# A Mamba-2 layer in split fp32: all weight splits at high priority, plain work inside the first Strassen pair, and another order of the scan's inserts

## The chip, the cores and the metric

The kernel runs on one core of one Trainium2 chip. The metric is the device time of one execution in microseconds (us). A core has a matmul engine (PE, or TensorE, with its weight load PEld), a vector engine (DVE), an activation engine (ACT), GpSimd (POOL) and SyncE (SP), which here mostly issues DMAs. Each engine runs its own instructions in a fixed order and waits on semaphores for the others.

## The reference

One Mamba-2 layer for 512 tokens and 2048 channels, with a final norm:

```python
hn   = rmsnorm(x, ln_g)
proj = hn @ w_in                        # 2048 -> z 4096, x 4096, B 1024, C 1024, dt 64
xbc  = silu(causal_conv4(x, B, C))
dt   = softplus(dt + dt_bias);  a = -exp(a_log)
# scan by chunks, 64 heads of 64 channels, 8 groups share B and C (128 states)
decay  = exp(where(mask, cs_l - cs_s, -inf));  cb = C @ B^T
y_diag = (cb * decay) @ (x * dt)
y_off  = (C @ state) * exp(cs)
state  = state * exp(last) + (B * w_in)^T @ (x * dt)
y = (y_diag + y_off + d_skip * x) * silu(z)
out = rmsnorm(x_in + rmsnorm(y, norm_g) @ w_out, final_g)
```

All inputs are float32.

## The kernel before, in words

**Splitting.** A float32 product is made of three matmuls on float32r parts: a weight piece arrives raw by DMA, ACT casts it to `hi` (L87) and DVE subtracts to get `lo` (L88); then hi*xh, hi*xl and lo*xh are summed in PSUM. The function is `split_piece`. Raw pieces lie in buffers `ra` (3), `rb` (1) and `rc` (2); `hi` and `lo` cycle through three buffers each, so a cast has to wait until PE is done with the piece three before it. A few splits have buffers of their own (`h1h`/`h1l` for R11, `oh`/`ol` in the out-projection).

**Stages.** First eight products ("plain": B0, C0, x0, z0, x1, z1, B1, C1) of 16 k-steps, in pieces of eight k-steps, through `mm_k` (L198). Then 36 *quads*: each computes two output tiles of the in-projection by a Strassen-Winograd scheme of seven half-size products, R11, T1, T2, R22, R21, T3 and T4, of 24 matmuls each (L635 to L637 for hi*xh, hi*xl, lo*xh). T1 is R12 fetched by DMA onto R11's raw buffer, T2 = T1 + R22 and T4 = T2 + R21 are made in place by DVE (L604), T3 is fetched onto R12. A quad's T4 product runs inside the next quad, behind T1: that place is called `prev`. Last come the out-projection's blocks: plain ones (`mm_o`, L929 to L931, 512 columns each, summed to `acc` by DVE at L1032), and two *chains* of four pairs each, `opair`, which use the same seven products (L867 to L869) on forms of y that `y_forms` makes on DVE (L841 to L848).

**The first pair of a chain.** The first quad, and the first pair of each out-projection chain, has no T4 of a predecessor for its `prev` place. There the order was another: T1, R11, nothing, R22, T2 (`lone`), and the events of the split moved with it.

**Order.** The code is traced in a loop of steps: a step is six matmuls (some 0.7 us), a quad is 28 steps. A table `ev` tells at which step a piece is loaded, split, added, or a part of the scan inserted; `add` fills it and `run` empties it. The order on PE, SP and POOL is the order in which the code was written and traced. The order on ACT and DVE is made by a scheduler, which takes what is ready in its own reckoning by priority; `with urgent():` gives instructions a high priority. Before, weight splits were urgent in the out-projection's pairs alone (L589).

**The scan.** For each of 32 units (two heads): `u_load` (DMA of decay rows), `u_decay` (ACT L456 to L459, then DVE L461 makes `m`), `u_xt` (transposes at L473, `xd` at L476, `xw` at L479), `u_state` (L488), `u_yd` (L502, L506, reads `m` and `xd`) and `u_yo` (L518 to L523). `g_bt` and `g_cb` prepare the groups (L416, L433 to L436). These are inserted between PE's steps. Around the start stand the token norm (L289 to L295), `dt` (L318 to L351) and `x_forms` (L549 to L578), which make the forms of x that the quads multiply with.

## Time and profile before

| what | value |
|---|---|
| median of 3 runs | 1290.69 us (1289.58 to 1293.99) |
| the profiled execution | 1295.7 us, its span 1294.0 us |
| granted PE clock, mean | 0.991 |
| PE busy | 1252.1 us (97%), 9932 matmuls |
| DVE busy | 1084.3 us (84%) |
| ACT busy | 826.6 us (64%) |
| POOL busy | 77.5 us (6%) |
| DMA | 225.90 MB, mean 175 GB/s |

The span is that of one execution, from its first to its last instruction. A row of the waits names the engine that stood still, its line and tile, and what ended its wait. A row of the timeline gives the start, the duration, the engine, the line, the operation, the tiles and, in brackets, the idle time before it. A row of the windows gives a stretch of the span, with the busy time of PE, PEld, DVE, ACT and POOL, and the clock that PE was granted. `L198 <- DVE lo L88` means a matmul of line 198 that waited for the difference of line 88.

### The profile page before, as it was taken

Reading aid. Unit: us, or ns where it says so; the run is one execution under the profiler, and the core shown is the slowest. Engines: PE = TensorE matmul, PEld = TensorE weight load, DVE = VectorE, ACT = ScalarE, POOL = GpSimd, SP = SyncE. Lnnn points to the kernel's source line nnn. Section 1 sums busy time; section 2 is a strip of 40 time slices with the busy share of each in tenths; the row PEclk is TensorE's granted clock in tenths of the full one; section 3 lists DMA queues with packets and bytes.
Section 4 is the critical chain, followed back from the end, with each engine's and each line's share of the span. In section 5 each row is a group of like instructions: output and inputs, shape, how many; then the busy total and the mean of one; then the engine's idle time right before and its main releaser. Section 6 shows DMA issues by size and latency. Waiting matters only on the chain.

```text
span 1294.0 us, 24519 instructions
## 1 busy us (share of the span) xinstructions
PE 1252.1 (97%) x9932; PEld 1192.9 (92%) x9932; DVE 1084.3 (84%) x1449; ACT 826.6 (64%) x1357; POOL 77.5 (6%) x99
## 2 busy tenths in 40 slices
PE   8989899999999999999999999999999899999997
PEld 8989899999999999999999999999988899899885
DVE  5796988988989898998889899889857877887865
ACT  7667667677666757767685867778666445434433
POOL 0000001010000101010100001000000000000000
PEclk9989999999999999999999999999999999999999
DMA  9546657585676667667667677766637576647612
GB/s 356 179 141 172 162 161 174 143 215 142 192 197 174 159 169 183 164 176 199 162 161 195 151 188 171 212 155 154 185 105 258 146 199 199 197 119 229 183 57 98
DMA packets 70194, 225.90 MB, mean 175 GB/s; under 512 B 8384, under 2 KB 12800, under 8 KB 69952
## 3 DMA queue, kind: packets, MB, share of 16 engines
q1 hardware_dynamic: 56688, 176.34, 40.2%
q0 software_dynamic: 12672, 46.14, 22.1%
q8 instruction: 78, 1.28, 0.4%
q10 hardware_dynamic: 720, 1.84, 0.4%
q14 instruction: 36, 0.29, 0.1%
HBM read 211.52 MB, written 12.78 MB: 173 GB/s over the span
## 4 chain that ended last, share of the span: by engine, by line
PE 74%; DVE 11%; DMA 7%; issue 4%; ACT 3%; SPq 0%; POOL 0%; DVEq 0%; ACTq 0%; POOLq 0%
PE S L637 7%; PE S L635 7%; PE S L636 7%; PE mm L635 5%; PE mm L636 4%; PE R L635 4%; PE mm L637 4%; PE R L636 4%; PE R L637 4%; DVE lo L88 3%; PE mm L929 3%; PE mm L931 3%; PE mm L930 3%; PE yd L502 2%; PE mm L867 2%
## 5 line engine op out<-in xcount | busy, mean ns | idle before, releaser
L87 ACT CAST hi<-ra 128x1024 fp32r<-128x1024 f32 x150 | 154.7, 1046 | 159.5 <-DVE ra L604 72.9
L88 DVE TENSOR_TENSOR lo<-ra,hi 128x1024 fp32r<-128x1024 f32 x150 | 181.3, 1221 | 24.2 <-ACT hi L87 24.1
L635 PE MATMUL mm<-xh,hi 128*128 128x256 f32 x576 | 163.6, 284 | 0.0
L637 PE MATMUL mm<-xh,lo 128*128 128x256 f32 x576 | 160.6, 279 | 0.6 <-DVE lo L88 0.6
L636 PE MATMUL mm<-xl,hi 128*128 128x256 f32 x576 | 160.4, 278 | 0.0
L637 PE MATMUL R<-s,lo 128*128 128x256 f32 x576 | 160.3, 278 | 0.1
L635 PE MATMUL R<-s,hi 128*128 128x256 f32 x576 | 160.2, 278 | 0.0
L636 PE MATMUL R<-s,hi 128*128 128x256 f32 x576 | 160.2, 278 | 0.0
L88 DVE TENSOR_TENSOR lo<-rc,hi 128x1024 fp32r<-128x1024 f32 x94 | 114.9, 1223 | 28.5 <-ACT hi L87 28.1
L87 ACT CAST hi<-rc 128x1024 fp32r<-128x1024 f32 x94 | 98.4, 1047 | 50.8 <-issue 29.1
L604 DVE TENSOR_TENSOR ra<-ra,rc 128x1024 f32<-128x1024 f32 x88 | 107.7, 1224 | 13.3 <-DMA rc<-in_wi 11.8
L635 PEld LDWEIGHTS mm<-xh,hi 128*128 128x128 f32 x576 | 108.1, 188 | 5.2 <-issue 5.0
L637 PEld LDWEIGHTS mm<-xh,lo 128*128 128x128 f32 x576 | 109.2, 190 | 0.8 <-DVE lo L88 0.8
L637 PEld LDWEIGHTS R<-s,lo 128*128 128x128 f32 x576 | 109.1, 189 | 0.3 <-DVE lo L88 0.3
L635 PEld LDWEIGHTS R<-s,hi 128*128 128x128 f32 x576 | 108.2, 188 | 0.0
L636 PEld LDWEIGHTS mm<-xl,hi 128*128 128x128 f32 x576 | 108.2, 188 | 0.0
L636 PEld LDWEIGHTS R<-s,hi 128*128 128x128 f32 x576 | 108.1, 188 | 0.0
L637 PE MATMUL S<-xh,lo 128*128 128x256 f32 x288 | 83.5, 290 | 5.6 <-DVE lo L88 5.6
L635 PE MATMUL S<-xh,h1h 128*128 128x256 f32 x288 | 83.4, 290 | 1.0 <-DVE xr L398 1.0
L635 PE MATMUL S<-xh,hi 128*128 128x256 f32 x288 | 81.3, 282 | 2.2 <-ACT xh L577 1.3
L636 PE MATMUL S<-xl,hi 128*128 128x256 f32 x288 | 81.2, 282 | 0.7 <-DVE xl L578 0.7
L636 PE MATMUL S<-xl,h1h 128*128 128x256 f32 x288 | 80.8, 280 | 0.0
(452 smaller groups left out, 3940.8 us busy)
## 6 DMA issues: line engine op xcount, KB each, us to landing
rc<-in_wi SPq DMA_DIRECT2D x76, 512.0 KB, 5.9
ra<-in_wi SPq DMA_DIRECT2D x42, 512.0 KB, 6.2
rb<-in_wi SPq DMA_DIRECT2D x40, 512.0 KB, 6.9
ra<-in_wi POOLq DMA_DIRECT2D x36, 512.0 KB, 6.3
rb<-in_wi POOLq DMA_DIRECT2D x36, 512.0 KB, 5.9
csb<-cscr SPq DMA_DIRECT2D x32, 512.0 KB, 8.0
ra<-in_wo SPq DMA_DIRECT2D x26, 512.0 KB, 5.4
yscr<-xs SPq DMA_DIRECT2D x32, 256.0 KB, 2.6
```

The lines of the kernel that those rows point to most:

```text
L87: S.copy(out=hi, in_=raw)
L88: V.tensor_tensor(out=lo, in0=raw, in1=hi, op=ALU.subtract)
L502: T.matmul(pyd[r, i, :], x[:, 2 * i, hh, :], m[:, i, hh::4, :], start=i == 0, stop=False, skip_group_check=True)
L604: V.tensor_tensor(out=raw, in0=raw, in1=qs[n][other], op=ALU.add)
L635: T.matmul(ps, hi[:, k, :], ah, start=first and k == 0, stop=False, skip_group_check=True)
L636: T.matmul(ps, hi[:, k, :], al, start=False, stop=False, skip_group_check=True)
L637: T.matmul(ps, lo[:, k, :], ah, start=False, stop=k == KH - 1, skip_group_check=True)
L867: T.matmul(ps[:, t, :], yh[:, k, tt], hi[:, k, :], start=st, stop=False, skip_group_check=True)
L929: T.matmul(ps, yh, hi, start=first and k == 0, stop=False)
L930: T.matmul(ps, yh, lo, start=False, stop=False)
L931: T.matmul(ps, yl, hi, start=False, stop=last and k == 1)
```

## The change

Three things are changed.

1. In `split_piece` the cast and the difference are now inside `urgent()`, for every weight piece of the kernel. (The lines are 89 and 90 there, and what follows is shifted by two to four lines.)
2. The first pair of a chain uses the same order as all others: R11, T1, `prev`, T2, R22, R21, T3. For `prev` it takes plain work: in the first quad the last four k-steps of the last plain product (so quads begin four steps earlier, `QB`), and in the out-projection the last two token tiles of the last piece of the block before the chain (`bridge`, made by `tail`, whose accumulate is L993). The offsets of `y_fetch` and `y_forms` for the first chain change, and the pieces that go to the pool's own buffers are those with n divisible by 4.
3. The events are added to the table in another order: within one step, yd now comes before `g_bt` and `g_cb`, and the state after them. On PE a steady insert `L488 L502 L506` becomes `L502 L506 L488` (in the lines of before).

```diff
--- before.py
+++ after.py
@@ -84,8 +85,9 @@
     def split_piece(raw, shape, pool, names=("hi", "lo"), bufs=None):
         hi = pool.tile(shape, F32R, name=names[0], bufs=bufs)
         lo = pool.tile(shape, F32R, name=names[1], bufs=bufs)
-        S.copy(out=hi, in_=raw)
-        V.tensor_tensor(out=lo, in0=raw, in1=hi, op=ALU.subtract)
+        with urgent():
+            S.copy(out=hi, in_=raw)
+            V.tensor_tensor(out=lo, in0=raw, in1=hi, op=ALU.subtract)
         return hi, lo
 
     def rsqrt_small(dst, ssq, pool, n, width, tag, bufs=1):
@@ -114,13 +116,14 @@
         seq.append((("x", u), ("z", u)))
     plain = [s for pair in (seq[0], seq[1], seq[2], seq[3]) for s in pair]
     quads = seq[NPL // 2:]
+    QB = NPL * KT - 4
     tile_of = {"z": 0, "x": 32, "B": 64, "C": 72}
     QS = 28
     at = {s: i * KT for i, s in enumerate(plain)}
     for i, pair in enumerate(quads):
         for s in pair:
-            at[s] = NPL * KT + i * QS
-    END = NPL * KT + len(quads) * QS
+            at[s] = QB + i * QS
+    END = QB + len(quads) * QS
     WSH = [P, 8, P]
     OSH = [P, 2, L]
 
@@ -140,6 +143,7 @@
     base = [END]
     for i, blk in enumerate(blocks):
         late = 4 if i == 0 or type(blocks[i - 1]) is tuple else 0
+        late -= 4 if type(blocks[min(i + 1, len(blocks) - 1)]) is tuple else 0
         base.append(base[-1] + (4 * QS if type(blk) is tuple else 8 * n_pieces(blk) + late))
 
     def wo_src(p, s):
@@ -160,7 +164,7 @@
     def get_out(n, name="ra"):
         if n < len(wo_order) and n not in opieces:
             opieces[n] = split_piece(load_piece(wo_src(*wo_order[n]), OSH, name), OSH,
-                                     *((op, ("oh", "ol")) if n % 4 == 3 else (wp,)))
+                                     *((op, ("oh", "ol")) if n and n % 4 == 0 else (wp,)))
 
 
     xh = xp.tile([P, KT, L], F32R, name="xh")
@@ -586,8 +590,7 @@
 
     def q_split(n, f, own=False):
         raw = qs[n][f]
-        with urgent() if n >= len(quads) else ExitStack():
-            qs[n, f] = split_piece(raw, WSH if n < len(quads) else QSH, wp, *((("h1h", "h1l"), 1) if own else ()))
+        qs[n, f] = split_piece(raw, WSH if n < len(quads) else QSH, wp, *((("h1h", "h1l"), 1) if own else ()))
 
     def q_load(n, f, half, tile_, name):
         qs.setdefault(n, {})[f] = load_piece(*q_src(n, half, tile_), name)
@@ -607,12 +610,11 @@
     qs = {}
     oquads = [blk for blk in blocks if type(blk) is tuple]
 
-    def q_events(n, b, last, e=0, t1=0, lone=False):
+    def q_events(n, b, last, e=0):
         for o, f, a in ((-38 - e, q_load, ("R11", 0, 0, "ra")), (-23 - e, q_split, ("R11", True)),
-                        (-23 - e, q_fetch, ("T1", "R11", 0, 1)), (-3 - e // 2 - t1, q_split, ("T1",)),
+                        (-23 - e, q_fetch, ("T1", "R11", 0, 1)), (-3 - e // 2, q_split, ("T1",)),
                         (-12 - e // 2, q_load, ("R22", 1, 1, "rc")), (1 - e // 2, q_add, ("T2", "T1", "R22")),
-                        *(((5, q_split, ("R22",)), (9, q_split, ("T2",))) if lone else
-                          ((5, q_split, ("T2",)), (9, q_split, ("R22",)))),
+                        (5, q_split, ("T2",)), (9, q_split, ("R22",)),
                         (-8, q_load, ("R21", 1, 0, "rc")), (12, q_add, ("T4", "T2", "R21")),
                         (13, q_split, ("R21",)),
                         (-7, q_load, ("R12", 0, 1, "rb")), (-7, q_fetch, ("T3", "R12", 1, 1)),
@@ -646,35 +648,17 @@
         W = lambda f: lambda: qs[n, f]
         A = ps_mm.tile([P, L], F32, name="mm")
 
-        def first(step):
-            product(s_, W("R11"), 11, True, step)
-            with urgent():
-                S.copy(out=A[:, lo_], in_=s_)
-
-        def second(step):
-            product(r_, W("T1"), 1, True, step)
-            with urgent():
-                S.copy(out=sn[:, 1, :], in_=r_)
-
-        if prev:
-            first(b)
-            second(b + 4)
-            prev(b + 8)
-        else:
-            second(b)
-            first(b + 4)
-            for i in range(8, 12):
-                run(b + i)
-        def third(step):
-            product(r_, W("R22"), 4, False, step)
-
-        def fourth(step):
-            product(s_, W("T2"), 2, False, step)
-            with urgent():
-                S.copy(out=sn[:, 0, :], in_=s_)
-
-        for f, step in zip((fourth, third) if prev else (third, fourth), (b + 12, b + 16)):
-            f(step)
+        product(s_, W("R11"), 11, True, b)
+        with urgent():
+            S.copy(out=A[:, lo_], in_=s_)
+        product(r_, W("T1"), 1, True, b + 4)
+        with urgent():
+            S.copy(out=sn[:, 1, :], in_=r_)
+        prev(b + 8)
+        product(s_, W("T2"), 2, False, b + 12)
+        with urgent():
+            S.copy(out=sn[:, 0, :], in_=s_)
+        product(r_, W("R22"), 4, False, b + 16)
         with urgent():
             V.tensor_tensor(out=zq[:, lo_], in0=r_, in1=sn[:, 0, :], op=ALU.add)
         product(A[:, lo_], W("R21"), 12, False, b + 20)
@@ -704,17 +688,23 @@
     def add(step, f, *a):
         ev.setdefault(step, []).append((f, a))
 
+    ramp = [[66, 71, 63, 75, 87, 92], [56, 65, 50, 68, 86, 92]]
+    steps = [ramp[u] if u < len(ramp) else [28, 42, 56, 65, 65, 71] for u in range(NU)]
+
+    def add_units(*kinds):
+        for u in range(NU):
+            for i, f in kinds:
+                add(at["x", u] + steps[u][i], f, u)
+
+    add_units((0, u_load), (1, u_decay), (2, u_xt))
+    add_units((4, u_yd))
     for g in range(1, G):
         add(at["B", g] + (30 if ("B", g) in plain else 93), g_bt, g)
         for i in range(2):
             add(at["x", 4 * g] + 28, g_cb, g, i)
-    ramp = [[66, 71, 63, 75, 87, 92], [56, 65, 50, 68, 86, 92]]
-    for u in range(NU):
-        w = ramp[u] if u < len(ramp) else [28, 42, 56, 65, 65, 71]
-        for o, f in zip(w, (u_load, u_decay, u_xt, u_state, u_yd, u_yo)):
-            add(at["x", u] + o, f, u)
+    add_units((3, u_state), (5, u_yo))
     for n in range(len(quads)):
-        q_events(n, NPL * KT + n * QS, n == len(quads) - 1, 0 if n else 14, lone=not n)
+        q_events(n, QB + n * QS, n == len(quads) - 1, 0 if n else 14)
     for i in range(4):
         add(49 + 7 * i, x_forms, i // 2, i % 2)
         add(114 + 4 * i, x_form3, i)
@@ -788,7 +778,7 @@
 
     for n in range(2, NPL):
         ps = None
-        for k in range(KT):
+        for k in range(KT if n < NPL - 1 else KT - 4):
             if k % 8 == 0:
                 get_piece(2 * n + k // 8 + 2)
             run(n * KT + k)
@@ -800,9 +790,15 @@
                 del pieces[2 * n + k // 8]
         if n == 2:
             st["x0"] = ps
-        else:
+        elif n < NPL - 1:
             finish(n, ps)
-    prev = None
+
+    def prev(step):
+        for i in range(4):
+            run(step + i)
+            mm_k(ps, pieces[2 * NPL - 1], 4 + i, KT - 4 + i)
+        finish(NPL - 1, ps)
+
     for n in range(len(quads)):
         prev = pair(n, prev)
 
@@ -878,36 +874,18 @@
         q0, q1 = acc[:, 0:2, c[1]], acc[:, 2:4, c[1]]
         A0 = ps_mm.tile([P, 2, LH], F32, name="mm")
 
...
+        oproduct(s_, i, W("R11"), 11, True, b)
+        with urgent():
+            S.copy(out=A0, in_=s_)
+        oproduct(r_, i, W("T1"), 1, True, b + 4)
+        with urgent():
+            V.tensor_tensor(out=q1, in0=q1, in1=r_, op=ALU.subtract)
+        prev(b + 8)
+        oproduct(s_, i, W("T2"), 2, False, b + 12)
+        with urgent():
+            V.tensor_tensor(out=q0, in0=q0, in1=s_, op=ALU.subtract)
+        oproduct(r_, i, W("R22"), 4, False, b + 16)
+        V.tensor_tensor(out=q0, in0=q0, in1=r_, op=ALU.subtract)
         oproduct(A0, i, W("R21"), 12, False, b + 20)
         V.tensor_tensor(out=p0, in0=p0, in1=A0, op=ALU.add)
         oproduct(s_, i, W("T3"), 3, False, b + 24)
@@ -963,10 +941,10 @@
     for i, blk in enumerate(blocks):
         if type(blk) is tuple:
             for s in range(4):
-                q_events(len(quads) + 4 * m + s, base[i] + s * QS, s == 3, 0, 3 if s == 0 else 0, s == 0)
+                q_events(len(quads) + 4 * m + s, base[i] + s * QS, s == 3)
             for j in range(2):
-                add(base[i] - ((50, 32), (54, 32))[m][j], y_fetch, m, j)
-                add(base[i] - ((39, 24), (47, 24))[m][j], y_forms, m, j)
+                add(base[i] - ((48, 30), (54, 32))[m][j], y_fetch, m, j)
+                add(base[i] - ((36, 23), (47, 24))[m][j], y_forms, m, j)
             m += 1
     sb = [i for i, blk in enumerate(blocks) if type(blk) is tuple]
     for i in range(16):
@@ -1006,6 +984,16 @@
                 step += QS
             m += 1
             continue
+        def tail(ps, w, y, t, s, first, step):
+            for k in range(2):
+                run(step + k)
+            mm_o(ps, w, y, t, first, True)
+            a = acc[:, t, s * L:(s + 1) * L]
+            with urgent():
+                V.tensor_tensor(out=a, in0=ps, in1=a, op=ALU.add)
+
+        bridge = []
+        n_end = n0 + n_pieces(blk)
         end = n0 + n_pieces(blk) + (n_pieces(blocks[kb + 1]) if kb + 2 < len(blocks) else 0)
         for s, pairs in blk:
             ps = [None] * NC
@@ -1018,6 +1006,9 @@
                     if p == pairs[0]:
                         ps[t] = first.pop(0) if first else (ps_o or (ps_s, ps_mm)[t % 2]).tile(
                             [P, L], F32, name="mm" if ps_o or t % 2 else "S")
+                    if type(blocks[kb + 1]) is tuple and s == 3 and n0 + 1 == n_end and t > 1:
+                        bridge.append(partial(tail, ps[t], opieces[n0], ys[p], t, s, p == pairs[0]))
+                        continue
                     if kb or n0 or t > 1:
                         for k in range(2):
                             run(step)
@@ -1043,6 +1034,10 @@
                     load_y(2)
                     fg = fp.tile([P, DM], F32, name="fg")
                     nc.sync.dma_start(fg, d["fg"].partition_broadcast(P))
+        if bridge:
+            def prev(step, parts=bridge):
+                for i, f in enumerate(parts):
+                    f(step + 2 * i)
 
 
     assert not ev, ev
```

The order on DVE shows what the scheduler makes of it. First, a quad behind a B/C pair, around the T3 difference (`lo<-rb`); L391 is the convolution, `m<-m,cbm` L461. Before:

```order
L88 TENSOR_TENSOR lo<-rc,hi 128x1024
L391 SCALAR_TENSOR_TENSOR xs<-xr,par,xs 128x512 x2
L461 TENSOR_TENSOR m<-m,cbm 128x1536
L391 SCALAR_TENSOR_TENSOR xs<-xr,par,xs 128x512
L679 TENSOR_TENSOR z<-R,sn 128x256
L88 TENSOR_TENSOR lo<-rb,hi 128x1024
L88 TENSOR_TENSOR lo<-ra,hi 128x1024
L604 TENSOR_TENSOR ra<-ra,rc 128x1024
```

Now (L395, L465 and L663 are what L391, L461 and L679 were):

```order
L90 TENSOR_TENSOR lo<-rc,hi 128x1024
L395 SCALAR_TENSOR_TENSOR xs<-xr,par,xs 128x512 x3
L90 TENSOR_TENSOR lo<-rb,hi 128x1024
L663 TENSOR_TENSOR z<-R,sn 128x256
L90 TENSOR_TENSOR lo<-ra,hi 128x1024
L607 TENSOR_TENSOR ra<-ra,rc 128x1024
L90 TENSOR_TENSOR lo<-ra,hi 128x1024
L465 TENSOR_TENSOR m<-m,cbm 128x1536
```

The T3 difference has moved ahead of `m<-m,cbm` and of the `z` that reads R. Second, the token norm at the start; `z<-ident,rtok` is made four times and read by PE at L294 (`tr`). Before:

```order
L102 TENSOR_TENSOR rtok<-rx_r,rx_t 128x4
L289 TENSOR_SCALAR z<-ident,rtok 128x128 x4
L88 TENSOR_TENSOR lo<-rb,hi 128x1024
L295 COPY rbc<-tr 128x512
L88 TENSOR_TENSOR lo<-rc,hi 128x1024
L88 TENSOR_TENSOR lo<-ra,hi 128x1024
```

Now:

```order
L104 TENSOR_TENSOR rtok<-rx_r,rx_t 128x4
L293 TENSOR_SCALAR z<-ident,rtok 128x128
L90 TENSOR_TENSOR lo<-rb,hi 128x1024
L90 TENSOR_TENSOR lo<-rc,hi 128x1024
L90 TENSOR_TENSOR lo<-ra,hi 128x1024
L293 TENSOR_SCALAR z<-ident,rtok 128x128 x3
L299 COPY rbc<-tr 128x512
```

Three of the four now stand behind three differences. Third, the first pair of the first out-projection chain, from the subtraction that follows T1 on; `ra<-ra,rc` is T2 = T1 + R22, then T4; L882, L886 and L888 of the change are L889, L907 and L902 of before. Before, from the addition on:

```order
L604 TENSOR_TENSOR ra<-ra,rc 128x1024
L952 SCALAR_TENSOR_TENSOR acc<-xt,rms,acc 128x512
L88 TENSOR_TENSOR h1l<-ra,h1h 128x1024
L88 TENSOR_TENSOR lo<-ra,hi 128x1024
L88 TENSOR_TENSOR lo<-rc,hi 128x1024
L88 TENSOR_TENSOR lo<-rb,hi 128x1024
L604 TENSOR_TENSOR ra<-ra,rc 128x1024
L902 TENSOR_TENSOR acc<-acc,mm 128x2x256
L88 TENSOR_TENSOR lo<-ra,hi 128x1024
L907 TENSOR_TENSOR acc<-acc,mm 128x2x256
```

Now:

```order
L882 TENSOR_TENSOR acc<-acc,mm 128x2x256
L837 TENSOR_TENSOR f22l<-yr,f22h 128x512
L993 TENSOR_TENSOR acc<-mm,acc 128x512
L607 TENSOR_TENSOR ra<-ra,rc 128x1024
L993 TENSOR_TENSOR acc<-mm,acc 128x512
L930 SCALAR_TENSOR_TENSOR acc<-xt,rms,acc 128x512
L90 TENSOR_TENSOR lo<-ra,hi 128x1024
L90 TENSOR_TENSOR lo<-rc,hi 128x1024 x2
L607 TENSOR_TENSOR ra<-ra,rc 128x1024
L886 TENSOR_TENSOR acc<-acc,mm 128x2x256
L90 TENSOR_TENSOR lo<-rb,hi 128x1024
```

The addition for T2 now stands behind the first accumulate of the moved plain work (L993), and the subtraction of T2's product (L886) ahead of the next `lo<-ra`.

More of the change, by code (lines that the diff above doesn't have):

```diff
@@ L1 @@
 from contextlib import ExitStack
+from functools import partial
 import numpy as np
@@ L639, in pair @@
     def pair(n, prev):
-        b = NPL * KT + n * QS
+        b = QB + n * QS
         (kp, ip), (kq, iq) = quads[n]
@@ L879, in opair @@
         A0 = ps_mm.tile([P, 2, LH], F32, name="mm")
-        def first(step):
-            oproduct(s_, i, W("R11"), 11, True, step)
-            with urgent():
-                S.copy(out=A0, in_=s_)
-        def second(step):
-            oproduct(r_, i, W("T1"), 1, True, step)
-            with urgent():
-                V.tensor_tensor(out=q1, in0=q1, in1=r_, op=ALU.subtract)
-        if prev:
-            first(b)
-            second(b + 4)
-            prev(b + 8)
-        else:
-            second(b)
-            first(b + 4)
-            for k in range(8, 12):
-                run(b + k)
-        def third(step):
-            oproduct(r_, i, W("R22"), 4, False, step)
-            V.tensor_tensor(out=q0, in0=q0, in1=r_, op=ALU.subtract)
-        def fourth(step):
-            oproduct(s_, i, W("T2"), 2, False, step)
-            with urgent():
-                V.tensor_tensor(out=q0, in0=q0, in1=s_, op=ALU.subtract)
-        for f, at_ in zip((fourth, third) if prev else (third, fourth), (b + 12, b + 16)):
-            f(at_)
+        oproduct(s_, i, W("R11"), 11, True, b)
[10 more added lines that the diff above has]
+        V.tensor_tensor(out=q0, in0=q0, in1=r_, op=ALU.subtract)
         oproduct(A0, i, W("R21"), 12, False, b + 20)
```

## Prediction

> **What bounds the kernel now.** I read first the page's busy table and its costliest groups, then the waits of PE.
>
> ```profile
> span 1294.0 us, 24519 instructions
> PE 1252.1 (97%) x9932; PEld 1192.9 (92%) x9932; DVE 1084.3 (84%) x1449; ACT 826.6 (64%) x1357; POOL 77.5 (6%) x99
> ...
> L87 ACT CAST hi<-ra 128x1024 fp32r<-128x1024 f32 x150 | 154.7, 1046 | 159.5 <-DVE ra L604 72.9
> ...
> L604 DVE TENSOR_TENSOR ra<-ra,rc 128x1024 f32<-128x1024 f32 x88 | 107.7, 1224 | 13.3 <-DMA rc<-in_wi 11.8
> ```
>
> PE is busy 97% of the span, and the change leaves its 9932 matmuls as they are. So the matmuls are the floor, and only PE's waits can move. A weight piece costs 1.05 us on ACT and then 1.2 us on DVE (rows below) before PE can use it. In PE's waits these lines bear on the change:
>
> ```profile
> PE S L637 <- DVE lo L88: 5.6, 9, 1.5
> PE S L198 <- DVE lo L88: 4.0, 1, 4.0
> PE mm L867 <- DVE acc L907: 2.5, 1, 2.5
> PE mm L869 <- DVE lo L88: 1.8, 2, 1.4
> PE mm L867 <- DVE acc L889: 1.7, 1, 1.7
> PE mm L930 <- DVE lo L88: 1.2, 1, 1.2
> PE tr L373 <- DVE xd L476: 1.0, 1, 1.0
> PE S L635 <- ACT hi L87: 0.9, 1, 0.9
> PE mm L867 <- ACT hi L87: 0.9, 1, 0.9
> PE S L636 <- DVE xl L578: 0.7, 1, 0.7
> PE mm L637 <- DVE lo L88: 0.6, 1, 0.6
> PE tr L473 <- DVE win L366: 0.6, 1, 0.6
> PE S L930 <- DVE lo L88: 0.5, 1, 0.5
> ```
>
> Columns are total us, times, longest. Most of these waits are for a difference (L88). The start (6.1 us for L181) comes before any of the changed work and stays.
>
> A wait can cost twice. These are stretches of the span, with the busy time of PE, PEld, DVE, ACT, POOL, then the granted PE clock:
>
> ```profile
> 73.50:76.90 3.40, 1.50 (x13) 1.29 (x11) 2.96 (x7) 1.54 (x3) 0.00 (x0) 1.00 0.00 0
> 77.00:80.40 3.40, 1.44 (x6) 1.44 (x7) 3.40 (x7) 0.52 (x1) 0.00 (x0) 0.50 0.53 129
> 80.40:83.80 3.40, 3.40 (x17) 3.40 (x17) 3.40 (x8) 2.47 (x5) 0.00 (x0) 0.50 0.98 371
> 165.70:169.10 3.40, 3.39 (x16) 3.39 (x17) 3.37 (x3) 0.59 (x1) 0.00 (x0) 0.50 0.66 193
> 1022.40:1025.80 3.40, 1.07 (x9) 1.10 (x10) 3.04 (x4) 1.28 (x2) 0.00 (x0) 1.00 0.86 312
> 1025.90:1029.20 3.30, 3.30 (x18) 3.30 (x17) 2.30 (x3) 0.08 (x1) 0.88 (x1) 0.50 0.36 83
> ```
>
> After a stretch of 3.4 us in which PE was busy for 1.5 or 1.07 us, the next stretch ran at a clock of 0.50; half of PE's busy time in it is lost. That is (1.44 + 3.40) / 2 = 2.4 us at 77, 1.7 at 166 and 1.65 at 1026. By these rows some 2 us of idle inside one such stretch is enough. The Trainium skill's "TensorE: Matmul & The Clock Gate" (Part 1) has a free-running window of 3413 ns, which agrees with the stretches' length, but speaks of a whole idle window, or gaps over 3.4 us, before the clock halves; no gap here but the 4.0 us one is that long, and the measured rows decide. By the page's rule the windows that I add below would not come (third rival).
>
> **Part 1: casts and differences go first.** In the quads after a B/C pair the T3 difference stood behind scan work:
>
> ```profile
> 497.25 1.05 ACT L87 CAST hi<-rb 128x1024 fp32r<-128x1024 f32 x1
> 497.50 1.75 DVE L461 TENSOR_TENSOR m<-m,cbm 128x1536 f32<-128x1536 f32 x1
> 500.16 1.21 DVE L88 TENSOR_TENSOR lo<-rb,hi 128x1024 fp32r<-128x1024 f32 x1
> 511.39 0.65 PE L502 MATMUL yd<-m,xd 128*64 128x256 f32 x4
> ```
>
> The cast is done at 498.3; the difference starts 1.9 us later, after L461 and two more. In the changed order it stands ahead of L461 and L679. L461 now comes behind two more differences and an addition as well, some 5 us later (4 x 1.2); the yd insert that needs it (L502) starts at 511.39, 12 us after its end of before. So the 5.6 + 0.6 us of L637's waits go, and the 0.9 of L635 for a cast of quad 1's T3, with its window at 166 (1.7): **-8.8 us**. Without that cover each of these nine waits would come back at L502 with up to 1.2 us: the bounds are -8.8 and +2.
>
> The same at plain work's piece 10, the largest single wait:
>
> ```profile
> 69.33 1.04 ACT L87 CAST hi<-rb 128x1024 fp32r<-128x1024 f32 x1
> 77.69 1.22 DVE L88 TENSOR_TENSOR lo<-rb,hi 128x1024 fp32r<-128x1024 f32 x1
> 81.64 1.05 ACT L87 CAST hi<-rc 128x1024 fp32r<-128x1024 f32 x1 [0.21 <-DMA rc<-in_wi]
> 84.44 1.23 DVE L88 TENSOR_TENSOR lo<-rc,hi 128x1024 fp32r<-128x1024 f32 x1
> ```
>
> Cast done at 70.4, difference at 77.7, behind the dt series on DVE. Now it follows the two L436: the 4.0 goes, and the 2.4 of clock: **-6.4**. What is late next is the following piece: its DMA sets its cast at 81.64, so with its difference directly behind, PE has it at about 84 (81.64 + 1.05 + 1.22). PE, 4.1 us earlier and at full clock, would want it at about 81.6. So **+2.4** comes back (bounds 0, if the DMA starts earlier by as much as the buffer comes free, to 4.0).
>
> **What the priority puts in front of others.** DVE and ACT run their queues in order, so an urgent instruction that waits holds what is behind it. Early places:
>
> ```profile
> 41.93 1.05 ACT L87 CAST hi<-ra 128x1024 fp32r<-128x1024 f32 x1 [1.39 <-PE mm L198]
> 39.77 0.88 DVE L289 TENSOR_SCALAR z<-ident,rtok 128x128 f32<-128x128 f32 x4
> 41.92 1.05 PE L294 MATMUL tr<-z,ones 128*128 128x128 f32 x8
> ```
>
> The four L289 were together and PE reached L294 at 41.92 without a wait. Now three of them stand behind three differences, the last of whose casts waits for PE till 41.93 and ends at 42.98. Then a difference and three L289 (1.2 + 0.7) follow: L294's last matmuls start no earlier than 44.9. They started by 42.5 (eight of them from 41.92): **+2.4** (0 to 3; it is plainly in the order).
>
> At L473, h1l and two lo differences now stand before the last L366: two by 1.13 more, 0.6 becomes about 2.3, while the 1.0 of L373 is covered by it: **+0.7** (-1 to 2.3).
>
> ```profile
> 110.83 1.76 DVE L461 TENSOR_TENSOR m<-m,cbm 128x1536 f32<-128x1536 f32 x1 [1.12 <-ACT m L459]
> 112.80 0.65 PE L502 MATMUL yd<-m,xd 128*64 128x256 f32 x4
> ```
>
> L502 came 0.2 us after L461's end. Two casts now stand ahead of L459, on which L461 waits: 2 x 1.05 at most, and PE arrives earlier too. I take **+1.1**, about half (0 to 2.1). In the first quad the x forms already make PE wait (0.7 for L578). R22's cast now waits for the plain work that was moved into the quad, and holds the forms behind it. I estimate **+0.7** (-2 to 3), by the row it is nearest to, the 0.7 of L578.
>
> Three of the new waits (L294, the piece after 10, the forms) are of some 2 us or more; by the clock rows I take two of them to fall into one window: **+3.4** (0 to 5.1).
>
> Twelve more table loads fall to ACT (six at L458, six at L690), 1.28 us each by the row below. They are 15 us of ACT, which is idle for 36% of the span: 0 (0 to 4, if three of them fall ahead of a cast that PE waits for). The Trainium skill ("ScalarE: Activation LUTs", What ACT_TABLE_LOAD costs) adds a drain of 1.38 us to each, which would make 32 us of ACT and still fit; no run here shows it.
>
> ```profile
> L394 ACT ACT_TABLE_LOAD x31 | 39.8, 1283 | 0.6
> ```
>
> **Part 2: the first pair of a chain.** In the first out-projection chain:
>
> ```profile
> 1022.76 1.23 DVE L88 TENSOR_TENSOR lo<-ra,hi 128x1024 fp32r<-128x1024 f32 x1 [2.06 <-ACT hi L87]
> 1023.90 0.68 DVE L907 TENSOR_TENSOR acc<-acc,mm 128x512 f32<-128x512 f32 x1
> ```
>
> L907, which frees the bank that T3 wants, stood behind a difference that idled 2.06 us for its cast. It now comes before that difference: -2.5, and its window -1.65. R22 no longer follows at once in the bank that T1 used, so the 1.7 for L889 in the second chain goes; the two L930 waits (1.2, 0.5) go since those pieces are urgent now and no longer behind the last pieces. Together **-7.5** (-8 to -3).
>
> T2 of that first pair stays late. In the new DVE order L604 stands behind the first accumulate of the moved plain work (L993 now), which ends 1.4 us after T1; then 0.7 + 1.2 (L604) + 1.05 (cast), another 0.7 and 0.7, and 1.2 for the difference, against 2.7 us of moved matmuls as cover. T2 waits about 3.0 us in two parts; before it was 1.8 + 0.9: **+0.3** (-2.7 to +2).
>
> **Part 3: yd first, state last.** The same matmuls in another order; matmuls are back to back, so only change-overs of about 0.1 us in 30 inserts differ: 0 (-3 to +3). The inserted state waits less for xw (L479), which covers the differences ahead of it.
>
> **The sum.** -8.8 - 6.4 + 2.4 + 2.4 + 0.7 + 1.1 + 0.7 + 3.4 - 7.5 + 0.3 = -11.7. The profiled execution took 1295.7 us (1.7 around its span): 1284.0. The median of the runs, 1290.69, is 5.0 below the profiled one, so I forecast **1279 us**.
>
> **Rivals.** (1) *Head of line on ACT* (slower). The casts hi<-ra wait 159.5 us in all, 72.9 of it for L604. With priority each may be fetched ahead of L456 to L459 of a unit and hold them while it waits for DVE or DMA; then L461 is late and PE stands at yd, in up to 30 units. It decides once the hold exceeds the slack of L461, which is 12 us at 500 but 0.2 us at 112.8. At 0.5 us a unit it is +15: 1279 + 15 = 1294. For it: the 2.06 us that L907 lost just so. Against it: T1 is fetched by a DMA that lands some 3 us before its cast's place. Chance 0.10. (2) *Waits change places*: PE's waits move to the next late thing, as with the piece behind 10, and the steady gain (8.8) is taken by L461 and the forms: 1279 + 8.8 + 2 = 1290. For it: DVE is 84% busy, and nothing there gets shorter. Chance 0.13. (3) *No new half-clock windows*: the waits are cut up, as with T2, and 3.4 goes from the sum: 1275.6; with T2 on time and the first piece landing early, 1270. For it: T2's late hi and lo (0.9 and part of the 1.8), cut in two, are followed by the full clock at 1022. By the page's rule above this would be the outcome. Chance 0.22. (4) My forecast, 1274 to 1285: chance 0.55.
>
> **The range**: 1267 to 1293. It leaves out the far half of rival 1 and sums of all lower bounds; the likeliest case alone is 1274 to 1285. About 0.3% (3.9 us) is what a measurement here can tell. Faster by more than that (below 1286.8) are cases 3 and 4, with a little of the others: 0.78. Same: most of rival 2, 0.13. Slower: 0.09.
>
> **What would show it.** Right: no wait of S L637 for L88 above 0.3 us in the steady quads; the 4.0 of S L198 gone and one of 2 to 2.5 us in its place at about 80; a new wait at L294 near 42; mm L867 no longer waiting for L907 and L889; T2 of the first out-projection pair waiting for its cast and difference for about 3 us. Wrong: a row of yd L502 waiting for L461 many times (rival 1), a steady wait of S L637 that only changes its releaser (rival 2), or no stretch at a clock of 0.50 before 200 us (rival 3).

## The result and the profile after

The changed kernel took 1333.82 us (median of 4, 1327.04 to 1337.85) against 1292.21 us of the kernel before on the same chip (1289.58 to 1293.99). The ratio is 1.0318, with a 95% interval of 1.0271 to 1.0366: it is slower by 3.2%. The forecast was 1279 us, so the sign was wrong.

The profiled execution of the changed kernel is the fastest of its four (1327.04 us), and that of the kernel before (1295.7 us) was slower than its median, so the two traces differ by 31 us where the medians differ by 42. The page of the changed kernel begins so:

```profile
span 1325.3 us, 24524 instructions
...
PE 1259.7 (95%) x9932; PEld 1190.0 (90%) x9932; DVE 1089.8 (82%) x1449; ACT 841.5 (63%) x1369; POOL 78.2 (6%) x99
...
PE 35%; DMA 27%; DVE 16%; ACT 14%; issue 6%; SPq 1%; POOL 0%; ACTq 0%; DVEq 0%; POOLq 0%
DMA csb<-cscr 10%; DVE lo L90 6%; DMA rb<-in_wi 5%; ACT hi L89 5%; DMA ra<-in_wi 4%; PE mm L907 3%; PE mm L908 3%; PE mm L909 3%; PE mm L863 3%; PE mm L865 3%; PE mm L864 3%; DMA rc<-in_wi 3%; ACT L462 2%; DVE m L465 2%; PE S L638 2%
```

The last two lines are the chain of work that ended last. For the kernel before, the same part of the page reads:

```profile
PE 74%; DVE 11%; DMA 7%; issue 4%; ACT 3%; SPq 0%; POOL 0%; DVEq 0%; ACTq 0%; POOLq 0%
```

PE does as many matmuls as before and was 74% of the chain. Now it is 35%, and DMA has gone from 7% to 27%: the loads of decay rows (`csb`) head the list, and weight pieces follow. That is the first sign that something holds the loads.

PE's waits in the changed kernel (engine, line, what it waited for; total, times, longest in us):

```profile
PE yo L522 <- DVE stsl L408: 6.6, 8, 1.4
...
PE S L907 <- ACT hi L89: 5.6, 1, 5.6
PE mm L637 <- ACT mm L668: 5.5, 6, 1.8
PE tr L477 <- ACT xs L398: 4.4, 7, 1.6
PE S L202 <- ACT hi L89: 3.3, 1, 3.3
PE S L637 <- ACT xh L581: 3.2, 1, 3.2
PE tr L298 <- DVE z L293: 2.8, 1, 2.8
PE S L639 <- DVE lo L90: 2.7, 8, 0.5
PE yd L506 <- DVE m L465: 2.6, 2, 2.0
...
PE mm L863 <- ACT hi L89: 1.9, 1, 1.9
...
PE mm L865 <- DVE lo L90: 0.8, 1, 0.8
```

The old waits that the change was to remove are gone or halved (S of the quads for `lo`: 5.6 to 2.7, the longest now 0.5; the 4.0 at piece 10; L907 and L889 of before). New ones have come at yo, at the transposes of x (L477), at the copy L668, and at the first piece of the out-projection (L907).

Where the time went, by stage. This table is worked out from the starts of PE's matmuls in the profiled executions (us from the first matmul; quads are counted from 0, and a quad's start is its first R11 matmul):

```
                                  to quad 4   quads 4-34   34 to end   to chain 1   chain 1 to last matmul   sum
before                              210.6       668.1        51.2         69.2           279.0             1278.1
changed                             212.5       688.7        61.2         72.3           274.7             1309.4
changed, store of y later           211.9       655.7        50.2         69.8           275.3             1262.9
before, store of y later            208.1       665.8        50.1         69.3           272.9             1266.2
before, part 3, store later         205.2       658.6        49.9         69.3           274.1             1257.1
parts 2 and 3, store later          206.7       657.9        49.8         66.6           275.9             1256.9
```

(In kernels with part 2, 2.7 us of plain matmuls move from "to chain 1" into the chain.) The part up to quad 4 is 1.9 us longer, and the one from the first chain on 4.3 us shorter. The loss lies between: 20.6 us in quads 4 to 34, 10.0 behind them and 3.1 before the first chain. Most of the 10.0 is one wait, the 5.6 us of the out-projection's first piece (L907), and the half clock behind it (0.53 and 0.50 granted from 958.5 to 965.4).

Both kernels' timelines around one and the same unit show what is late there. Its last yo matmul is shown first, then DVE's rows. Before:

```profile
474.23 0.28 PE L520 MATMUL yo<-csth,stsl 128*128 128x256 f32 x1
...
474.74 0.42 DVE L521 TENSOR_TENSOR ecs<-yo,ecs 128x256 f32<-128x256 f32 x1
...
475.73 0.42 DVE L522 TENSOR_TENSOR xs<-xs,ecs 128x256 f32<-128x256 f32 x1
...
476.73 0.68 DVE L523 TENSOR_TENSOR xs<-xs,z 128x512 f32<-128x512 f32 x1
```

Now:

```profile
484.42 0.28 PE L524 MATMUL yo<-csth,stsl 128*128 128x256 f32 x1
...
486.34 1.21 DVE L90 TENSOR_TENSOR lo<-rc,hi 128x1024 fp32r<-128x1024 f32 x1
...
488.26 0.41 DVE L525 TENSOR_TENSOR ecs<-yo,ecs 128x256 f32<-128x256 f32 x1
...
489.78 1.23 DVE L90 TENSOR_TENSOR lo<-rb,hi 128x1024 fp32r<-128x1024 f32 x1
...
491.59 0.68 DVE L527 TENSOR_TENSOR xs<-xs,z 128x512 f32<-128x512 f32 x1
```

The unit's last product, y*z (L523 before, L527 now), starts 2.5 us after the last yo matmul before, and 7.2 us after it now; two urgent differences and what they push back lie between. Over the 32 units the mean lag is 2.89 us before and 7.73 us now. The store of y waits for y*z at the head of SP's queue. Before:

```profile
477.44 0.33 SPq L524 DMA_DIRECT2D yscr<-xs  x1
477.87 0.37 SPq L81 DMA_DIRECT2D rc<-in_wi  x1
...
479.74 0.70 SPq L440 DMA_DIRECT2D csb<-cscr  x1
```

Now:

```profile
492.30 0.33 SPq L528 DMA_DIRECT2D yscr<-xs  x1
492.73 0.37 SPq L82 DMA_DIRECT2D rc<-in_wi  x1
...
494.60 0.70 SPq L444 DMA_DIRECT2D csb<-cscr  x1
```

Everything behind the store goes out as soon as it has gone: two `rc` pieces, an `ra`, an `rb`, and the decay rows. Against the unit's yo, `csb` is issued at 479.74 - 474.2 = 5.5 us before and at 494.60 - 484.4 = 10.2 us now. On ACT the first decay instruction then waits for it, before and now:

```profile
488.95 0.40 ACT L456 ACTIVATE m<-csb,cs 128x128 f32<-128x128 f32 x1 [0.71 <-DMA csb<-cscr]
...
504.37 0.40 ACT L460 ACTIVATE m<-csb,cs 128x128 f32<-128x128 f32 x1 [1.71 <-DMA csb<-cscr]
```

Over the whole execution ACT's waits for these rows grow from 4.9 us in 6 places to 35.6 us in 21 (total, times, longest; before, then now):

```profile
ACT m L456 <- DMA csb<-cscr: 4.9, 6, 1.8
...
ACT m L460 <- DMA csb<-cscr: 35.6, 21, 3.6
```

This is still only a reading. The experiments test it.

### The profile page after: what moved, and what is told of

Its sections match the earlier page's. It is cut to its first block, busy times and chain, and to the rows that moved or that the text cites. A ratio compares the mean times of both kernels' runs of the same rounds, so it can differ in the third digit from the quotient of the medians.

```text
span 1325.3 us, 24524 instructions
## 1 busy us (share of the span) xinstructions
PE 1259.7 (95%) x9932; PEld 1190.0 (90%) x9932; DVE 1089.8 (82%) x1449; ACT 841.5 (63%) x1369; POOL 78.2 (6%) x99
## 3 DMA queue, kind: packets, MB, share of 16 engines
q8 instruction: 78, 1.28, 0.4%
q10 hardware_dynamic: 720, 1.84, 0.3%
## 4 chain that ended last, share of the span: by engine, by line
PE 35%; DMA 27%; DVE 16%; ACT 14%; issue 6%; SPq 1%; POOL 0%; ACTq 0%; DVEq 0%; POOLq 0%
DMA csb<-cscr 10%; DVE lo L90 6%; DMA rb<-in_wi 5%; ACT hi L89 5%; DMA ra<-in_wi 4%; PE mm L907 3%; PE mm L908 3%; PE mm L909 3%; PE mm L863 3%; PE mm L865 3%; PE mm L864 3%; DMA rc<-in_wi 3%; ACT L462 2%; DVE m L465 2%; PE S L638 2%
## 5 line engine op out<-in xcount | busy, mean ns | idle before, releaser
L89 ACT CAST hi<-ra 128x1024 fp32r<-128x1024 f32 x153 | 159.7, 1045 | 147.6 <-DVE ra L607 75.8
L90 DVE TENSOR_TENSOR lo<-ra,hi 128x1024 fp32r<-128x1024 f32 x153 | 186.7, 1221 | 54.2 <-ACT hi L89 52.8
L639 PE MATMUL S<-xh,h1l 128*128 128x256 f32 x288 | 80.7, 280 | 0.0
```

Of the source, the lines that this page charges most:

```text
L89: S.copy(out=hi, in_=raw)
L90: V.tensor_tensor(out=lo, in0=raw, in1=hi, op=ALU.subtract)
L639: T.matmul(ps, lo[:, k, :], ah, start=False, stop=k == KH - 1, skip_group_check=True)
```

## The experiments

Three theories stood against each other. **A**: the priority makes y*z late, the store of y waits for it in SP's queue, and the loads behind the store come late. **B** and **C**: part 3 or part 2 makes the loss. **D**: DVE and ACT are simply too full of urgent work, and SP's queue has no part in it. Every ratio below is against the kernel before on the same chip, with its 95% interval. Medians of two experiments can come from two chips, where the kernel before took 1292 to 1295 us.

### Part 1 alone

```diff
-        S.copy(out=hi, in_=raw)
-        V.tensor_tensor(out=lo, in0=raw, in1=hi, op=ALU.subtract)
+        with urgent():
+            S.copy(out=hi, in_=raw)
+            V.tensor_tensor(out=lo, in0=raw, in1=hi, op=ALU.subtract)
```

> The kernel before with part 1 alone (cast and difference urgent for every weight piece). Theory A (the priority pushes a unit's last product y*z, L523, back on DVE; the store of y waits for it in SP's queue, and the loads and decay rows queued behind the store come late): slower by 25 to 40 us, y*z starts 7 to 8 us after the unit's last yo matmul as in the changed kernel (7.73 us mean there, 2.89 before). Theory B (the state last makes yo wait for its split state and so y late): within 8 us of before, lag about 3 us. Theory C (the first pairs' new order costs it): within 8 us of before.

Measured: 1338.87 us, ratio 1.0354 (1.0330 to 1.0379); lag of y*z 7.25 us. The lag is as theory A said; the loss, 44.7 us, is above its 25 to 40. The priority alone makes a loss as large as the whole change.

### Without part 1

In the changed kernel `split_piece` is put back (no `urgent()` around the cast and the difference), and pairs of the out-projection are urgent as before:

```diff
+        with urgent() if n >= len(quads) else ExitStack():
             qs[n, f] = split_piece(raw, WSH if n < len(quads) else QSH, wp, ...)
```

> The changed kernel without part 1 (parts 2 and 3 stay). Theory A: not slower than before, 1283 to 1295 us, lag of y*z about 3 us. Theory B: slower than before by 20 us or more, lag 7 us. Theory C: slower by 10 us or more, the loss in the first quad and in the out-projection.

Measured: 1310.91 us, ratio 1.0139 (1.0111 to 1.0167); lag 4.39 us. No theory had this right: parts 2 and 3 lose 16.7 us of their own, and the lag is a third of the way from 2.89 to 7.73. Theory C had the size, but not the place: up to quad 4 it takes 208.0 us (210.6 before), and the loss is in quads 4 to 34 (680.7 against 668.1). So a part of B is true as well.

### The changed kernel, with y urgent too

```diff
+        with urgent():
             V.tensor_tensor(out=ecs, in0=pyo, in1=ecs, op=ALU.mult)
             V.tensor_tensor(out=y[:, 2 * P:L], in0=y[:, 2 * P:L], in1=ecs, op=ALU.add)
             V.tensor_tensor(out=y, in0=y, in1=z, op=ALU.mult)
```

> The changed kernel with the three DVE operations behind yo (ecs, the sum, y*z) urgent too. Theory A: the lag of y*z falls to 2 to 4 us and most of the steady quads' 22 us comes back: 1300 to 1312 us. If DVE is simply too full of urgent work (theory D: the waits of PE in the quads come from DVE and ACT directly, not by SP's queue): the lag falls but the time stays above 1322 us.

Measured: 1291.91 us, ratio 0.9984 (0.9974 to 0.9994); lag 3.55 us. Three short DVE instructions in each of 32 units, put ahead, take back some 42 us. It came out better than A's range. The order on SP is that of the changed kernel.

### The changed kernel, with the store of y later in SP's queue

```diff
     def u_yo(u):
...
-        nc.sync.dma_start(yscr[u // UPG][:, u % UPG, :], y)
...
+    for u in range(NU):
+        add(at["x", u] + steps[u][5] + 8, u_store, u)     # u_store(u): the same dma_start
```

> The changed kernel with the store of y issued as an event of its own eight steps (some 5.4 us) later in SP's queue, behind the piece loads of that place; y*z itself stays late. Theory A, with the queue as the carrier: 1300 to 1315 us, lag of y*z still 7 us or more. Theory D: no change, 1325 to 1338 us.

Measured: 1282.46 us, ratio 0.9919 (0.9900 to 0.9938); lag of y*z 6.39 us. Here y is still late, if less than the 7 us or more that A expected, and its store stands behind the piece loads. The time falls by 51 us against the changed kernel, to well below A's 1300 to 1315. The priority is still there, so D is out as the cause of the loss. One thing moves along with the store: the scheduler makes another order on DVE and ACT (at least 183 of DVE's 1449 instructions and 141 of ACT's 1286 stand elsewhere than in the changed kernel), and no run holds that order fixed. So that SP's queue carries the loss rests on this edit and the one before it together, and on the waits. SP's waits in the changed kernel, then in the one with the store later, where L519 is the store:

```profile
SPq L528 <- DVE xs L527: 495.1, 26, 24.9
SPq L82 <- DVE lo L90: 225.8, 43, 19.5
SPq L528 <- DVE z L663: 109.2, 6, 19.4
```

```profile
SPq L82 <- DVE lo L90: 666.2, 122, 22.4
SPq L519 <- DVE xs L531: 153.9, 32, 22.1
```

In the first, SP mostly waits at the store (both rows of L528 are waits of the store, 604.3 us in 32 places), and the loads behind have to wait with it. In the second it mostly waits for the buffers of the loads themselves (`lo` done means that a raw piece is free). ACT's waits for the decay rows fall from 35.6 us to 10.2:

```profile
ACT m L460 <- DMA csb<-cscr: 10.2, 8, 4.2
```

### Part 2 alone, part 3 alone, and the later store in the kernel before

The first has the change's edits of `QB`, `q_events`, `pair`, `opair`, `get_out`, `bridge` and `y_fetch`, and nothing else. The second has this one alone:

```diff
+    add_units((0, u_load), (1, u_decay), (2, u_xt))
+    add_units((4, u_yd))
     for g in range(1, G): ...            # g_bt, g_cb
-    for u in range(NU):
...
-        for o, f in zip(w, (u_load, u_decay, u_xt, u_state, u_yd, u_yo)):
-            add(at["x", u] + o, f, u)
+    add_units((3, u_state), (5, u_yo))
```

The third is the kernel before with the `u_store` of above.

> The kernel before with part 2 alone (plain work in the first pair of each chain, its events and the pool's buffers). Parts 2 and 3 together took 1.4% more. If part 3 (yd first, state last) made that loss: 1285 to 1296 us, lag of y*z 2.9 us as before. If part 2 made it: 1303 to 1315 us, with PE's losses at the chains and at the out-projection's start.

Measured: 1295.33 us, ratio 1.0005 (0.9981 to 1.0030); lag 2.86 us. Part 2 is worth nothing by itself.

> The kernel before with part 3 alone. If the state last delays the unit's y: 1300 to 1315 us, lag of y*z 4 to 5 us in the steady quads (4.39 with parts 2 and 3, 2.89 before), SP's store late by as much and PE's waits for differences (S L637 for L88) more than 15 us. If part 2 made the loss: within 5 us of before, though the lag may be longer.

Measured: 1309.59 us, ratio 1.0121 (1.0082 to 1.0160); lag 4.54 us, and 12.9 us of S for L88, where more than 15 was expected. So part 3 makes the loss that was left without part 1, and again the lag has grown: the state comes later, so yo's split state (`stsl`) and y*z come later.

> The kernel before with the store of y eight steps later, nothing else. In it y*z came 2.9 us after yo. If the store at the head of SP's queue already cost before: faster, 1280 to 1288 us, with fewer waits of S L637 for L88. If the place of the store matters only once y is late: within 4 us of before.

Measured: 1282.31 us, ratio 0.9917 (0.9891 to 0.9944); lag 2.88 us. SP's first wait in the kernel before is the same one:

```profile
SPq L524 <- DVE xs L523: 549.3, 32, 19.0
```

Even with y on time, this move of the store is worth some 10 us. The table of stages says where: of the 11.9 us between the two profiled executions 2.5 lie up to quad 4, 2.3 in quads 4 to 34 and 1.1 behind them, and 6.1 from the first chain on, where no y of a unit is stored any more. In that chain the waits for L907 and for T2 are gone and the matmuls come closer together (see the last section). How the place of the store brings that is not shown; here, too, the scheduler's order changes with the edit (at least 55 instructions on DVE, 78 on ACT). Against this kernel, the changed one with the same later store (1282.46) has gained nothing.

### Early plain pieces at ordinary priority

The changed kernel with `u_store`, and:

```diff
-        with urgent():
+        with urgent() if first else ExitStack():      # plain pieces: first = n >= 10
             S.copy(out=hi, in_=raw)
             V.tensor_tensor(out=lo, in0=raw, in1=hi, op=ALU.subtract)
```

> The changed kernel with the store eight steps later, and with the first ten plain pieces split at ordinary priority again (pieces 10 to 15 and all later ones stay urgent). The wait of 2.2 us at the token norm's transposes (L298) should go and the 4.0 us at piece 10 stay away: 1276 to 1281 us. If the pieces after it only wait instead: 1281 to 1285 us, as with the store alone (1282.5).

Measured: 1282.04 us, ratio 0.9914 (0.9882 to 0.9945), as with the store alone. The wait at L298 went, but the one at the pieces after it was 3.3 us (2.3 with all pieces urgent), and L506 waited 2.1 us instead of 1.0. The waits changed places.

### Priority, and part 3, each with the later store

The kernels of part 1 alone and of part 3 alone, each with the `u_store` of above.

> The kernel before with part 1 and the store of y eight steps later. By the sum of the prediction the priority is worth -8.8 in the steady quads, once nothing in SP's queue waits for the late y: at least 4 us under the store alone (1282.3), 1272 to 1279. If the priority gives nothing even then (its waits only change places: the token norm, x, the start of the out-projection): 1281 to 1290 us. The store alone left PE 1.2 us of waits of S for L88, so there is little left to gain by it.

Measured: 1285.32 us, ratio 0.9933 (0.9910 to 0.9955); lag 6.40 us. The store alone gave 1282.31. So the priority earns nothing, even with the queue free: it removes the wait of 3.7 us at piece 10 and half of the 1.2 us for `lo` in the quads, and brings these:

```profile
PE tr L474 <- ACT xs L395: 4.6, 7, 1.6
PE S L199 <- ACT hi L88: 3.8, 1, 3.8
PE yd L503 <- DVE m L462: 3.1, 2, 1.8
...
PE tr L295 <- DVE z L290: 2.2, 1, 2.2
```

> The kernel before with part 3 and the store eight steps later. In the profiles the quads' matmuls of 256 columns come at one of two pitches, about 113.5 or 117.8 ns; an insert that ends with yd often leaves the longer one, and one that ends with the state the shorter one. If the order of part 3 sets the pitch: the mean pitch in the quads falls from 115.65 (store alone) to 113.5 to 114.3 ns, and the time to 1271 to 1278 us, 5 to 11 under the store alone (1282.3). If the pitch has another cause (the priority, which the kernel with all parts and the later store has too): 115 ns or more, and 1280 to 1286 us.

Measured: 1274.89 us (1274.55 to 1275.33), ratio 0.9868 (0.9838 to 0.9898); lag 4.15 us, mean pitch of the quads' matmuls 114.08 ns against 115.65 ns with the store alone. Part 3 gains 7.4 us by the medians, 6.3 by the ratios (the two kernels ran on two chips), once its late y blocks nothing, and the pitch moved as the expectation said. More on it below.

### A little priority

The kernel with part 3 and the later store, and:

```diff
+        with urgent() if first else ExitStack():
             S.copy(out=hi, in_=raw)
             V.tensor_tensor(out=lo, in0=raw, in1=hi, op=ALU.subtract)
...
+            split_piece(..., first=n >= 10)                               # plain pieces
+            split_piece(..., first=n >= len(quads) or f == "T3")          # quads and pairs
```

> As the kernel with part 3 and the later store, and urgent are, beside the out-projection's pairs as before, only T3 in the quads and the plain pieces from the tenth on. If the wait of 3.7 us at piece 10 and its half clock go without a new one: 3 to 7 us under the kernel with part 3 and the later store. If the pieces behind it wait instead: within 2 us of it.

Measured: 1286.90 us, ratio 0.9952 (0.9933 to 0.9971): 12 us slower than without that priority, which neither expectation had. In the profiled execution (1282.05 us, the fastest of its ten) one new wait makes most of the difference:

```profile
PE yd L503 <- DVE m L462: 7.7, 1, 7.7
```

Its lag of y*z is 5.49 us; to the start of the quads it takes 128.1 us, against 117.4 without the priority.

### Parts 2 and 3 with the later store

The kernel without part 1, with `u_store`.

> The changed kernel without part 1 and with the store of y eight steps later: parts 2 and 3 and the store. With all three parts it was 1282.5, with part 3 alone and the store 1274.9. If the priority is what costs those 7.6 us and part 2 is worth its gain of some 3 us in the first quad (seen with part 2 alone): 1268 to 1275 us. If part 2 costs them: 1279 to 1285 us.

Measured: 1274.44 us (1271.57 to 1275.93), ratio 0.9849 (0.9817 to 0.9880). Part 2 is again worth nothing (1274.89 without it), and the priority costs 8 us (1282.46 with it). This kernel and the one with part 3 and the later store beat both the kernel before and the changed one, by 1.3 to 1.5% against the former.

All medians together, each with its own kernel before in the ratio:

| parts | store as before | store eight steps later |
|---|---|---|
| none | 1292 to 1295 us | 1282.3 (0.9917) |
| 1 | 1338.9 (1.0354) | 1285.3 (0.9933) |
| 2 | 1295.3 (1.0005) | not run |
| 3 | 1309.6 (1.0121) | 1274.9 (0.9868) |
| 2, 3 | 1310.9 (1.0139) | 1274.4 (0.9849) |
| 1, 2, 3 | 1333.8 (1.0318) | 1282.5 (0.9919) |

The row of part 1 is the argument in one line: the same priority costs some 45 us with the store at its old place and 3 with the store later, and those 3 are within the intervals. By the stages, what it costs beside parts 2 and 3 with the later store is not in the steady quads: 5.2 us up to quad 4 and 3.2 before the first chain are lost, and 2.2 are gained in quads 4 to 34.

## Why the prediction was wrong

**The step that failed** is "-8.8 us" for the casts and differences that go first, with its bounds "-8.8 and +2". It looked at one instruction that is put back, L461, found 12 us of cover there, and stopped. L523 stood in the same rows of DVE's order in other quads, just ahead of the T3 difference, and it too was put back. Its cover was not looked up, and it has none: the store of y waits for it at the head of SP's queue, with two `rc` pieces, `ra`, `rb` and the decay rows behind. In place of a gain, quads 4 to 34 brought +20.6, and what stands behind them +10.0, most of it by the late first piece of the out-projection. With the store out of the way the same part of the program took 655.7 us instead of 665.8, so a gain of that size in the quads was there, but by the runs most of it is part 3's (658.6 with part 3, the store and no priority).

**Part 3 at "0 (-3 to +3)"** failed as well, on both sides. It costs 14.6 us in the kernel before, where the state last goes with a y that is later by 1.65 us (4.54 against 2.89). It gains 6 to 7 us with the store out of the way.

**The beginning** came out near the sum, in part by luck: forecast +1.7 up to the first quads (the terms of the beginning, less 2.6 for quad 1's wait and window), measured +1.9. Term by term: L298 waits 2.8 us (2.4 forecast); the piece after 10 waits 3.3 and 0.5 (2.4); L506 waits 2.0 (1.1; its other 0.5 comes later); the forms 3.2, 0.2 more than before (0.7). The waits for L366 and `xd` near 95 us, which were to grow by 0.7, went from 1.6 to 0.5, and a wait of 1.6 for x at L477, at 172.7 us, was in no term. The half-clock windows came: each of the two stretches quoted here is followed by one (columns as in the prediction).

```profile
40.50:43.90 3.40, 0.90 (x9) 0.71 (x7) 3.40 (x5) 2.83 (x3) 0.00 (x0) 1.00 0.01 2
43.92:47.33 3.41, 3.16 (x15) 3.16 (x16) 1.99 (x7) 0.00 (x0) 0.00 (x0) 0.50 0.00 0
84.87:88.28 3.41, 0.99 (x6) 0.79 (x7) 2.85 (x7) 2.59 (x3) 0.00 (x0) 1.00 0.95 371
88.29:91.70 3.41, 3.41 (x17) 3.32 (x16) 3.05 (x5) 3.40 (x6) 0.00 (x0) 0.50 0.49 198
```

PE was busy for 0.9 and 0.99 us of the first stretch of each pair, and the next stretch ran at 0.50. As before, some 2.4 us of idle inside one stretch was enough; the third rival (no new windows) is out. Laid on the grid of 3.413 us that the clock records show, all fourteen profiled executions agree: each of the 56 stretches at full clock with 1.84 us or more of idle PE was followed by one at 0.50, and none with less than 1.65 us was. The rule of the Trainium skill ("TensorE: Matmul & The Clock Gate", Part 1), by which the clock halves after a whole idle window, does not hold here.

**The chains** came out as worked out in sum. From the first chain to the end the forecast was -7.5 + 0.3 = -7.2, or -6.7 without the 0.5 us of L930, which stood at 931 us, before the chain; measured is -4.3, and 2.7 us of matmuls had moved in, so -7.0. T2 of the first pair was to wait "about 3.0 us in two parts": it waits 1.9 + 0.8 (L863 and L865 above). The 1.2 us of L930 went. The 0.5 did not: the first piece of the out-projection now waits 5.6 us (L907). Its load, too, stands behind a store of y. Luck helped the sum: the mean pitch of the matmuls (last section) fell from 117.5 to 113.8 ns in the first chain and rose from 113.8 to 117.8 in the second, about 2.5 us each way, and no term had either.

**The rivals.** The second (waits change places, 1290 us) has the mechanism that the runs with the later store show: there the priority removes its waits and brings others of the same sum. The first (head of line, 1294 us) named the right kind of thing at the wrong queue: ACT before yd, where SP before the loads was the place. L506 waited only 2.6 us in all. No case had the size. The chance given to slower, 0.09, was too small: the sum had a price for what goes first, but for only some of what goes back, and L523 was not among it.

**What stays open.** Why the medians with the priority and the later store are 3 to 12 us above those without it is shown only as the waits and stages listed. Part 2 is worth nothing by two pairs of runs, and where its gain goes is shown in part: in the kernel with part 2 alone the way from the first chain on takes 279.8 us against 279.0, so with the moved 2.7 taken off it is only 1.9 shorter, and the way to the first chain is some 4 us longer although the 2.7 moved out of it. PE waits 3.0 us for a cast at the out-projection's plain matmuls just before the chain and 2.8 for casts in the chains, and 17.0 us around them run at half clock, against 3.4 before.

## What to carry to other kernels

When some instructions are given priority, list those that move back, and follow each to the queue that waits for it; a store that waits for a computed result makes everything behind it in its DMA queue wait for that result. Look there first: SP's wait for y (32 times, 549.3 us) stood in the profile of the kernel before, and moving that one store eight steps back, the only edit, was worth 10 us (the scheduler's order moved with it). And an order of priority that removes the waits in sight may only exchange them; here the two fastest kernels are those without the added priority.

## What the runs showed of the hardware

The quads' matmuls of 256 columns come at one of two pitches, some 113.5 ns or some 117.8 ns, and stay with one for tens of microseconds. In the kernel before, at one insert (PE's timeline):

```profile
241.93 0.28 PE L635 MATMUL R<-s,hi 128*128 128x256 f32 x1
...
244.76 0.28 PE L636 MATMUL mm<-xl,hi 128*128 128x256 f32 x1
...
245.33 0.60 PE L488 MATMUL yo<-xw,bt 128*128 128x128 f32 x4
245.86 0.65 PE L502 MATMUL yd<-m,xd 128*64 128x256 f32 x4
...
249.54 0.28 PE L635 MATMUL S<-s,hi 128*128 128x256 f32 x1
...
251.66 0.28 PE L518 MATMUL yo<-csth,stsh 128*128 128x256 f32 x1
```

From 241.93 to 244.76 there are 25 matmuls, 113 ns each; behind the insert, from 249.54 to 251.66, there are 18, 118 ns each. Counted over PE's matmuls in the quads, at the longer pitch and at the shorter:

```
                                    longer   shorter   mean pitch, ns
before                               2806      3023        115.49
changed                              1470      4332        114.49
before, store of y later             3032      2820        115.65
part 1, store later                  1570      4300        114.54
part 3, store later                   935      4897        114.08
parts 2 and 3, store later           1063      4773        114.17
parts 1 to 3, store later             447      5406        113.70
```

Inserts change it. In the kernel before, of 14 inserts of the kind `state, yd` that began at the shorter pitch 5 ended at the longer one, and none the other way; in the kernel with all parts and the later store, all 6 inserts of the kind `yd, state` that began at the longer pitch ended at the shorter one. The transposes of x (L473) went back to the shorter one too, in 9 of 12 cases of the kernel before. At 4.3 ns a matmul, 2097 fewer of the longer ones (3032 less 935, both with the store later) are 9.0 us, somewhat more than part 3 gains (6 to 7). That pair shows that the order of an insert moves the pitch. It is not all that does: with part 1 and the order of before the count falls from 3032 to 1570 while the time does not fall, and the two chains, where nothing of the scan is inserted, stood at either pitch. Each count is from one execution, and what in PE holds the pitch is not shown.

The table loads of ACT took 1.28 us each, and the next instruction came at once; the drain of 1.38 us that the Trainium skill ("ScalarE: Activation LUTs", What ACT_TABLE_LOAD costs) adds to each is not in this trace. In the changed kernel's ACT timeline:

```profile
943.49 1.28 ACT L462 ACT_TABLE_LOAD   x1
944.79 0.40 ACT L462 ACTIVATE m<-csb,nwl 128x128 f32<-128x128 f32 x1
```
